# A decoder block with its first query's rope moved into the pair slots, and three other changes of order

## The chip, the cores and the metric

The kernel runs on one core of one Trainium2 chip. The metric is the device time of one execution in microseconds. The kernel before was timed in three runs: median 942.23 us, lowest 941.05, highest 942.41. A profiler's trace of one further execution comes with it. TensorE multiplies matrices, VectorE and ScalarE work on elements, GpSimd (POOL in the profile) does a little of both, and SyncE (SP) only issues transfers. Each engine works through its own list of instructions in order and waits at semaphores for the others.

## The reference, cut to what matters

One layer on x of 1024 positions by 1024 channels, all in float32. A modulated RMSNorm gives h; one input projection of h is split into parts; two branches are gated, projected, merged, projected again and added to x; a last RMSNorm ends it.

```python
h = rmsnorm(x, norm_g) * (1.0 + scale) + shift          # scale, shift, gate = c @ w_ada + b_ada
q, k, v, g_attn, xr, g_rnn, m_attn, m_rnn = split(h @ w_in)
q, k = partial_rope(q, positions), partial_rope(k, positions)   # 16 of 64 channels turned
y_attn = sliding_window_attention_with_sinks(q, k, v, sinks) * silu(g_attn)   # 16 heads, 4 kv heads, window 128
xr = causal_depthwise_conv(xr, conv_w, conv_b)                    # width 4
y_rnn = rg_lru(xr, positions, wa, ba, wx, bx, lam) * silu(g_rnn)  # a linear scan over positions
merged = sigmoid(m_attn) * (y_attn @ w_attn_proj) + sigmoid(m_rnn) * (y_rnn @ w_rnn_proj)
out = rmsnorm(x + gate * (merged @ w_out), final_g)
```

## The kernel before, in words

**Precision.** TensorE's fast float32 format keeps fewer bits than float32. So each operand is split into a high part (a cast, on ScalarE: `cast`, line 101 or, with a scale, 103) and a low part (the operand minus the high part, on VectorE: `rest`, line 107 or 109). A product is three matmuls: high by high, low by high, high by low. In the profile `wh` and `wl` are the two parts of a weight; `hh`, `hl` and `nh`, `nl` those of h and of differences of its blocks.

**Start.** Norm and modulation give h transposed, in eight chunks of 128 channels (`kc`). Three column blocks of the input projection (`starts`: two blocks of k, one of the first query q 0) are accumulated meanwhile. From there to the end of the attention the order is written by hand: the instructions of each engine run in the order of the Python code. Behind the start come: rope of the k blocks (`rope_a` for the block with the turned channels, `rope_b` for the other), the product for v (`v_product`, its results stored by `v_store`), the rope of the third start block, the split of the weights `rq[1]` of the second half of q 0, the operands `nh`, `nl` (`make_operands`), and the product of the second half of q 0 (`ps_q`), which needs both halves of those weights (`wq`).

**Pairs and slots.** The remaining columns of the input projection are 23 pairs of column blocks, in the order of the list `pairs`: Q[1], MA[0], Q[2], MA[1], Q[3], XR[0], and so on (Q: queries, MA and MR: merge gates, XR: the recurrent branch, GA and GR: SiLU gates). A pair is computed by Strassen's scheme: seven block products instead of eight, one in each of seven slots, every product 12 matmuls of 128x128 by 128x512 (line 506). Pair i starts at slot 7 i. `Pair.place` writes down in which slots the pair's other steps are issued: four transfers of weights from six slots before its start; sums of weight blocks (`tsum`) and the splits (`hi` on ScalarE, `lo` on VectorE) from two slots before; evacuations of the four PSUM banks; and the results' own steps (`sinks`: for a query, rope and stores to the DRAM tensors `q_d`; for gates, tanh and stores). A split is written one slot ahead of the product that uses it or earlier. `at_slot` appends steps to the list of a slot (`fixed`), so that in one slot the steps of the earlier pair stand ahead of those of the later one. Rope is two ScalarE copies of 32 rows and a VectorE product (f1), a product and a sum of 64 rows (f2), a cast (`rhi`) and a subtraction (`rlo`), the last two also for blocks that are not turned; then two stores on SP's queue.

**Background.** Work that no slot needs is kept in two waiting lists and issued by `background` when a planner's account of ScalarE and VectorE time (each step carries its estimated costs, `Load`) has room in the slot. `slots(n)` in such a list holds it for n slots. The first list has the gate row (`gate_row`: eight pieces of `w_gate`, multiplied and added on VectorE, summed by TensorE) and then the steps behind the recurrent gates (`after_gates`: sigmoids a1, a2, d1, d2, tanh a3, a4, a5, d3, root a6, d4, scan d5, d6, a7, d7; a is ScalarE, d VectorE). The second has the preparation of v (`v_prep`, four groups) and then the convolutions. There are four recurrent blocks (`hb` 0 to 3) with two halves each; in `start_gates` a `slots(1)` stands behind each step for hb 0 to 2, and behind step 0 alone for hb 3. The gate products of the recurrent blocks are inserted between slots on TensorE (`extra`).

**Attention and output.** The 32 blocks of attention start in slot 155, with the last pair and the first output projections as filling work. After them the written order ends, and the compiler's scheduler orders the rest by its own estimate of times, with program order as priority: the projection of the attention output with the merge, the preparation of the output weights (`load_wo`: load, multiply by the gate, split; `wo[k]` for k 0 to 7, with two buffers for the loaded piece), and the output product. For the first three of the eight output tiles the product (`out_k`, line 1511, six matmuls for a tile and a k) runs in chunks of k.

Of the kernel before, what the change touches and what calls it, by code (L numbers as in the profile page):

```python
# [23 lines left out]
S = 1024  # L24
D = 1024
# [26 lines left out]
def tile_hybrid_block(ctx, tc, x, pk, rows, posr, posi, invf, c_row, w_ss, w_gate, w_main, w_v,  # L52
# [42 lines left out]
    def slot():  # L95
        return (wp.tile([P, HALF], F32R, tag="wh", name="wh", bufs=5),
                wp.tile([P, HALF], F32R, tag="wl", name="wl", bufs=5))
# [14 lines left out]
    def split(dst, src, scale=1.0):  # L112
        cast(dst, src, scale)
        rest(dst, src, scale)
        return dst
# [271 lines left out]
    def make_operands(i):  # L387
        for t in (i, i + 4):
            nl[t] = hx.tile([P, S], F32R, tag="X", name="nl")
            A.copy(nh[t][:], xT[t][:])  # L390
            V.tensor_tensor(out=nl[t][:], in0=xT[t][:], in1=f32(nh[t][:]), op=ALU.subtract)
        NT1.append((nh[i][:, SL[0]], nl[i][:, SL[0]]))
        NT3.append((nh[i][:, SL[1]], nl[i][:, SL[1]]))
        NT4.append((nh[i + 4][:, SL[0]], nl[i + 4][:, SL[0]]))
        T2.append((nh[i + 4][:, SL[1]], nl[i + 4][:, SL[1]]))
# [56 lines left out]
    def now(*lists):  # L452
        for steps in zip(*lists):
            for st_ in steps:
                st_[3]()
# [27 lines left out]
    def slots(d):  # L483

        t = []

        def f():
            t.append(W["slot"])
            return W["slot"] >= t[0] + d
        return f  # L490

    def at_slot(t, *steps):

        for i, st_ in enumerate(steps):
            for one in st_ if isinstance(st_, list) else [st_]:
                fixed.setdefault(t + i, []).append(one)


    SLOT, GATE = 2.75, 5.5

# [9 lines left out]
    class Pair:  # L510
        def __init__(self, c, sinks, scale=1.0):
            self.c, self.sinks, self.scale = c, sinks, scale

        def place(self, s, par, last):

            b1, b2, b3 = bk[0], bk[1 + par], bk[3]
            R, O, sc = {}, {}, self.scale
            self.ops, self.banks = O, (b1, b2, b3, bk[2 - par])

            def load(n):  # L520
                i, j = int(n[1]) - 1, int(n[2]) - 1
                return "S", 0, 0, lambda: R.__setitem__(
                    n, load_half(w_main[self.c + i][:, SL[j]]))

            def tsum(dst, a, b, op):
                def f():
                    R[dst] = wp.tile([P, HALF], F32, tag="ws", name="ws", bufs=3)[:]
                    V.tensor_tensor(out=R[dst], in0=R[a], in1=R[b], op=op)  # L528
                return "D", 0, 0.69, f

            def hi(n):
                def f1():
                    O[n] = slot()
                    cast(O[n], R[n], sc)
                return "A", 0.62, 0, f1

            def lo(n):
                return "D", 0, 0.69, lambda: rest(O[n], R[n], sc)

            SUB, ADD = ALU.subtract, ALU.add  # L540
            at_slot(s - 6, [load("A11"), load("A21")], load("A22"), load("A12"))
            at_slot(s - 2, [hi("A11"), tsum("S1", "A21", "A22", ADD)],
                    [hi("S1"), lo("A11"), tsum("S2", "S1", "A11", SUB)],
                    [lo("S1"), tsum("S3", "A21", "A11", SUB)],
                    hi("S2"),
                    [hi("A12"), lo("S2"), tsum("S4", "S2", "A12", SUB)],
                    [hi("S4"), lo("A12")], [hi("S3"), lo("S4")], lo("S3"))
            at_slot(s + (5 if last else 7), hi("A22"), lo("A22"))

            T_ = {}  # L550

            def keep(n, src):
                def f():
                    T_[n] = stp.tile([P, HALF], F32, tag=n, name=n)
                    A.copy(T_[n][:], src)
                return "A", 0.58, 0, f

            at_slot(s + 1, ("A", 0.58, 0, lambda: A.copy(b1, b2)))
            at_slot(s + 2, keep("p5", b3))
            at_slot(s + 4, keep("u2", b2))  # L560
            at_slot(s + 5, *self.sinks["C11"](lambda: b1))

            def join(out_, n, a, b):
                def f():
                    T_[n] = out_()
                    V.tensor_tensor(out=T_[n], in0=a(), in1=b(), op=SUB)
                return "D", 0, 0.69, f

            d12, k12 = self.sinks["C12"]
            d22, k22 = self.sinks["C22"]  # L570
            at_slot(s + 6, join(d12, "C12", lambda: T_["u2"][:], lambda: b3),
                    *k12(lambda: T_["C12"]))
            at_slot(s + 7, join(d22, "C22", lambda: b2, lambda: T_["p5"][:]),
                    *k22(lambda: T_["C22"]))
            if last:
                def add():
                    V.tensor_tensor(out=T_["u2"][:], in0=T_["u2"][:], in1=self.banks[3], op=ADD)
                at_slot(s + 7, keep("u2", b2), ("D", 0, 0.69, add),
                        *self.sinks["C21"](lambda: T_["u2"][:]))
            else:  # L580
                at_slot(s + self.sinks.get("late", 10), *self.sinks["C21"](lambda: b2))
# [40 lines left out]

    def place(pairs):
        for i, p in enumerate(pairs):
            p.place(7 * i, i % 2, i == len(pairs) - 1)

    def run(pairs, extra):

# [126 lines left out]
    def start_gates(hb):  # L755

        load1, split1 = gate_weights(hb, 1)
        c0, c1 = after_gates(hb, 0), after_gates(hb, 1)
        waiting[0].append(lambda: ask(hb, 0))
        one, two = [], [lambda: ask(hb, 1)]  # L760
        for todo, steps_ in ((one, c0), (two, c1)):
            for i, step in enumerate(steps_):
                todo.extend(step + ([slots(1)] if hb < 3 or i == 0 else []))
                if todo is one and i == 1:
                    todo.append(lambda: second(hb))
        if hb == 3:
            one.insert(0, lambda: W.setdefault("rush", True))
        waiting[0].extend(one + two)
        waiting[1].extend([load1, slots(2)] + split1)
        return True  # L770
# [89 lines left out]
    def gate_row():  # L860
# [7 lines left out]
        def start():  # L868
            t["acc"] = gm.tile([P, D], F32, name="acc")
            load(0)  # L870
            load(1)
# [55 lines left out]
                                   op1=ALU.add)  # L927
            V.memset(pcol(PK_NG, 0), 1.0)

        start()  # L930
        waiting[0].append(slots(5))
        todo = [[("A", 1.5, 0, lam_a)], [("D", 0, 1.0, lam_0)]]
        todo += [[("D", 0, 1.05, lambda j=j: [lam_j(j - i) for i in range(3)])]
                 for j in (8, 5, 2)]
# [9 lines left out]
    def v_prep(g):  # L944
        t = {}
        vpp = W["vpp"]

        def f0():
            t["v"] = vpp.tile([P, 8, 64], F32, tag="v32", name="v32")
            dma(t["v"][:], v_d[:, :, g, :])  # L950

        def f1():
            t["d"] = vpp.tile([P, 8, 64], F32, tag="d32", name="d32")
            V.tensor_tensor(out=t["d"][:, 1:8, :], in0=t["v"][:, 1:8, :],
                            in1=t["v"][:, 0:7, :], op=ALU.subtract)
            V.tensor_copy(t["d"][:, 0, :], t["v"][:, 0, :])

        def f2():
            for n_ in ("vs", "dv"):
                t[n_] = vpp.tile([P, 8, P], F32R, tag=n_, name=n_)  # L960
            A.copy(t["vs"][:, :, 0:64], t["v"][:])
            A.copy(t["dv"][:, :, 0:64], t["d"][:])

        def f3():
            for n_, d_, dst in (("v", "vs", vs_d), ("d", "dv", dv_d)):
                V.tensor_tensor(out=t[d_][:, :, 64:128], in0=t[n_][:],
                                in1=f32(t[d_][:, :, 0:64]), op=ALU.subtract)
                dma(dst[g], t[d_][:])

        waiting[1].extend([[("S", 0, 0, f0)], slots(4 if g else 7), [("D", 0, 0.85, f1)],  # L970
                           [("A", 1.24, 0, f2)], [("D", 0, 1.38, f3)]])


# [320 lines left out]
    def part(i, rope, dst):  # L1294
        return [rope(lambda hf=hf: starts[i][1][hf], hf, dst) for hf in range(2)]
# [1 line left out]
    now(*part(0, rope_a, k_d))  # L1297
    v_product(bk[:2], 0)
    now(*part(1, rope_b, k_d))
    now(*part(2, rope_a, q_d[0]))  # L1300
    ps_v = new_ps()
    v_product(ps_v, 1)
    wq.append(split(slot(), rq[1], 0.125))
    v_store(bk[:2], 0)
    make_operands(0)
    make_operands(1)
    begin(-4, -3, -2)
    make_operands(2)
    v_store(ps_v, 1)
# [2 lines left out]
    ps_q = new_ps()  # L1312
    for kc in range(KC):
        mm_k(ps_q, wq, kc)
    now(*[rope_b(lambda hf=hf: ps_q[hf], hf, q_d[0]) for hf in range(2)])
    T.matmul(bk[0], hh[0][0][:, 0:P], hh[0][0], start=True, stop=True)
    b12_ctx.close()
    Load.act = Load.dve = 0.0
# [229 lines left out]
    for t in range(3):  # L1548
        load_x(t)
    first = [new_ps() for _ in range(3)]  # L1550
    for lo, hi in ((0, 4), (4, 8)):
        for t in range(3):
            for k in range(lo, hi):
                out_k(first[t], t, k)
# [91 lines left out]
```

## Time and profile before

| | |
|---|---|
| Median of three runs | 942.23 us |
| Lowest, highest | 941.05, 942.41 us |
| The profiled execution | 944.67 us |
| Its span, from first to last instruction | 942.9 us |
| Mean granted TensorE clock | 0.995 |
| TensorE busy | 910.3 us (97%) |
| VectorE busy | 688.4 us (73%) |
| ScalarE busy | 532.3 us (56%) |
| GpSimd busy | 109.1 us (12%) |
| DMA, mean over the span | 174 GB/s |

Times in the rows of a profile are microseconds from the start of the span. In a row of instructions stand the start, the duration, the engine, the source line, the operation, what it writes and reads with their shapes, and in brackets the time that the engine sat idle before it and what it waited for. Matmuls are pipelined: the time between two starts is what one costs, not its duration. PEld is the loading of weights, SPq SyncE's issuing of transfers. PEclk is the share of full clock that TensorE was granted.

### The profile page before, as it was taken

Reading aid. Unit: us, or ns where it says so; the run is one execution under the profiler, and the core shown is the slowest. Engines: PE = TensorE matmul, PEld = TensorE weight load, DVE = VectorE, ACT = ScalarE, POOL = GpSimd, SP = SyncE. Lnnn points to the kernel's source line nnn. Section 1 sums busy time; section 2 is a strip of 40 time slices with the busy share of each in tenths; the row PEclk is TensorE's granted clock in tenths of the full one; section 3 lists DMA queues with packets and bytes.
Section 4 is the critical chain, followed back from the end, with each engine's and each line's share of the span. In section 5 each row is a group of like instructions: output and inputs, shape, how many; then the busy total and the mean of one; then the engine's idle time right before and its main releaser. Section 6 shows DMA issues by size and latency. Waiting matters only on the chain. (4 is left out here: it accounts for less than half of the span.)

```text
span 942.9 us, 12429 instructions
## 1 busy us (share of the span) xinstructions
PE 910.3 (97%) x4261; PEld 753.2 (80%) x4261; DVE 688.4 (73%) x1068; ACT 532.3 (56%) x1038; POOL 109.1 (12%) x161
## 2 busy tenths in 40 slices
PE   5899989999999999999999999999999999998997
PEld 3689777788888888888887877888888888887886
DVE  8977798876668974986687675899999736656522
ACT  7434655454557755775687685888878622212311
POOL 1056000000000000000000001354454300000000
PEclk9999999999999999999999999999999999999999
DMA  8924565753323451354235348996655186436321
GB/s 318 364 68 155 181 223 201 268 181 130 115 79 122 144 181 34 124 176 155 71 134 190 100 152 266 325 350 210 215 186 175 57 323 225 164 126 211 124 78 67
DMA packets 81140, 164.20 MB, mean 174 GB/s; under 512 B 12771, under 2 KB 29155, under 8 KB 81078
## 3 DMA queue, kind: packets, MB, share of 16 engines
q1 hardware_dynamic: 77590, 155.06, 47.9%
q0 software_dynamic: 2192, 6.00, 2.0%
q10 hardware_dynamic: 1296, 2.36, 0.7%
q8 instruction: 33, 0.54, 0.2%
q14 instruction: 29, 0.24, 0.1%
HBM read 114.00 MB, written 49.78 MB: 174 GB/s over the span
## 5 line engine op out<-in xcount | busy, mean ns | idle before, releaser
L506 PE MATMUL bk<-nh,wl 128*128 128x512 f32 x368 | 144.6, 393 | 2.8 <-DVE wl L107 2.7
L506 PE MATMUL bk<-nh,wh 128*128 128x512 f32 x368 | 144.2, 392 | 0.0
L506 PE MATMUL bk<-nl,wh 128*128 128x512 f32 x368 | 143.8, 391 | 0.0
L107 DVE TENSOR_TENSOR wl<-r,wh 128x512 fp32r<-128x512 f32 x108 | 79.4, 739 | 17.8 <-ACT wh L101 17.8
L101 ACT CAST wh<-r 128x512 fp32r<-128x512 f32 x108 | 66.4, 619 | 33.5 <-DMA r<-w_ap 12.5
L506 PEld LDWEIGHTS bk<-nh,wl 128*128 128x128 f32 x368 | 69.5, 189 | 19.4 <-DVE wl L107 4.5
L506 PEld LDWEIGHTS bk<-nh,wh 128*128 128x128 f32 x368 | 69.4, 188 | 15.4 <-ACT wh L103 0.9
L506 PEld LDWEIGHTS bk<-nl,wh 128*128 128x128 f32 x368 | 69.5, 189 | 14.2
L506 PE MATMUL bk<-hh,wl 128*128 128x512 f32 x184 | 71.8, 390 | 1.1 <-DVE wl L107 1.1
L506 PE MATMUL bk<-hh,wh 128*128 128x512 f32 x184 | 71.6, 389 | 0.0
L506 PE MATMUL bk<-hl,wh 128*128 128x512 f32 x184 | 71.6, 389 | 0.0
L59 POOL DMA_DIRECT2D yh_d<-yh x1 | 0.6, 583 | 480.4 <-ACT yh L845 480.4
L107 DVE TENSOR_TENSOR wl<-ws,wh 128x512 fp32r<-128x512 f32 x80 | 54.4, 686 | 1.9 <-ACT wh L101 1.9
L101 ACT CAST wh<-ws 128x512 fp32r<-128x512 f32 x80 | 48.4, 614 | 5.9 <-DVE ws L528 4.6
L1050 ACT ACTIVATE p<-p,small 128x129 f32<-128x129 f32 x128 | 50.1, 401 | 0.0
L506 PEld LDWEIGHTS bk<-hh,wl 128*128 128x128 f32 x184 | 34.5, 188 | 8.9 <-DVE wl L107 1.9
L506 PE MATMUL bk<-hha,wl 128*128 128x512 f32 x92 | 36.1, 393 | 5.2 <-DVE wl L107 3.7
L506 PEld LDWEIGHTS bk<-hh,wh 128*128 128x128 f32 x184 | 34.5, 188 | 7.2
L506 PEld LDWEIGHTS bk<-hl,wh 128*128 128x128 f32 x184 | 34.5, 188 | 7.1
L1026 PE MATMUL s_ps<-ks,qs 128*128 128x256 f32 (+1 forms) x256 | 37.6, 289 | 0.2 <-DVE p L1040 0.2
L1528 ACT ACTIVATE o<-xo 128x1024 f32<-128x1024 f32 (+2 forms) x10 | 8.9, 889 | 48.7 <-DVE xo L1527 48.7
L506 PE MATMUL bk<-hla,wh 128*128 128x512 f32 x92 | 35.8, 389 | 0.0
(356 smaller groups left out, 2260.3 us busy)
## 6 DMA issues: line engine op xcount, KB each, us to landing
r<-w_main SPq DMA_DIRECT2D x100, 256.0 KB, 4.2
wada<-w_ss SPq DMA_DIRECT2D x16, 512.0 KB, 8.1
qs<-q_d SPq DMA_DIRECT2D x16, 512.0 KB, 5.5
ks<-k_d SPq DMA_DIRECT2D x24, 192.0 KB, 3.8
xt<-x SPq DMA_DIRECT2D x8, 512.0 KB, 7.0
q_d<-rhi SPq DMA_DIRECT2D x16, 256.0 KB, 3.7
q_d<-rlo SPq DMA_DIRECT2D x16, 256.0 KB, 3.0
wg<-w_gate SPq DMA_DIRECT2D x8, 512.0 KB, 5.6
```

What stands on the lines that cost most here:

```text
L59: return eng.dma_start(dst, src)
L101: A.copy(dst[0][:], src)
L107: V.tensor_tensor(out=dst[1][:], in0=src, in1=f32(dst[0][:]), op=ALU.subtract)
L506: W["pe"] = T.matmul(ps, ww[:, c], b[kc][xx_], start=(first and kc == 0 and i == 0), stop=(kc == 3 and i == 2), skip_group_check=not first)
L1026: W["pe"] = T.matmul(o, qs[:, j, qc], ks[:, b, k0 + (0 if n else P):k0 + 256], start=(b == 0), stop=(b == 1))
L1050: A.activation(px[:, j, :], px[:, j, :], AF.Exp, bias=sm[:, 0, j:j + 1], accum_out=sm[:, 1, j:j + 1])
L1528: A.activation(o[:, sl], xo[:, sl], AF.Square, accum_out=fs[:, i:i + 1])
```

## The change

Five edits, all of them of order. The third start block's rope is not run at once; its two halves are copied out of PSUM (two ScalarE copies) and their rope steps are put in slots 1 to 5; the rope of the second half of q 0 goes to slots 5 to 7. The split of `rq[1]` moves behind the first stores of v and two calls of `make_operands`. The weight steps of a pair that follows a query (pairs 1, 3 and 5) are put in front of what their slots hold (`ahead`). The gate row's first transfers are issued four slots later, and its first step waits three slots more instead of five in all; v's first transfer is four slots later and its wait four instead of seven. In the last recurrent block a `slots(1)` stands behind steps 0, 3 and 5 of the first half and 0, 3, 5 and 7 of the second. The first three output tiles go in chunks of k 0-1, 2-3 and 4-7 instead of 0-3 and 4-7.

```diff
+    def ahead(t, *steps):
+        for i, st_ in enumerate(steps):
+            fixed.setdefault(t + i, [])[:0] = st_ if isinstance(st_, list) else [st_]
...
-        def place(self, s, par, last):
+        def place(self, s, par, last, put_):
...
-            at_slot(s - 2, [hi("A11"), tsum("S1", "A21", "A22", ADD)],
+            put_(s - 2, [hi("A11"), tsum("S1", "A21", "A22", ADD)],
...
-            p.place(7 * i, i % 2, i == len(pairs) - 1)
+            p.place(7 * i, i % 2, i == len(pairs) - 1,
+                    ahead if i and pairs[i - 1] in Q else at_slot)
...
-                todo.extend(step + ([slots(1)] if hb < 3 or i == 0 else []))
+                gap = hb < 3 or i in ((0, 3, 5) if todo is one else (0, 3, 5, 7))
+                todo.extend(step + ([slots(1)] if gap else []))
...
-        start()
-        waiting[0].append(slots(5))
+        waiting[0].extend([slots(4), [("S", 0, 0, start)], slots(3)])
...
-        waiting[1].extend([[("S", 0, 0, f0)], slots(4 if g else 7), [("D", 0, 0.85, f1)],
+        waiting[1].extend(([] if g else [slots(4)]) + [
+                           [("S", 0, 0, f0)], slots(4), [("D", 0, 0.85, f1)],
...
-    now(*part(2, rope_a, q_d[0]))
+    kept = [blk(), blk()]
+    for hf in range(2):
+        A.copy(kept[hf], starts[2][1][hf])
+        at_slot(hf + 1, *rope_a(lambda hf=hf: kept[hf], hf, q_d[0]))
     ps_v = new_ps()
     v_product(ps_v, 1)
-    wq.append(split(slot(), rq[1], 0.125))
     v_store(bk[:2], 0)
     make_operands(0)
     make_operands(1)
+    wq.append(split(slot(), rq[1], 0.125))
...
-    now(*[rope_b(lambda hf=hf: ps_q[hf], hf, q_d[0]) for hf in range(2)])
+    for hf in range(2):
+        at_slot(hf + 5, *rope_b(lambda hf=hf: ps_q[hf], hf, q_d[0]))
...
-    for lo, hi in ((0, 4), (4, 8)):
+    for lo, hi in ((0, 2), (2, 4), (4, 8)):
```

More of the change, by code (lines that the diff above doesn't have):

```diff
@@ L541, in place @@
             at_slot(s - 6, [load("A11"), load("A21")], load("A22"), load("A12"))
-            at_slot(s - 2, [hi("A11"), tsum("S1", "A21", "A22", ADD)],
[L543 to L547, printed above, removed]
+            put_(s - 2, [hi("A11"), tsum("S1", "A21", "A22", ADD)],
+                 [hi("S1"), lo("A11"), tsum("S2", "S1", "A11", SUB)],
+                 [lo("S1"), tsum("S3", "A21", "A11", SUB)],
+                 hi("S2"),
+                 [hi("A12"), lo("S2"), tsum("S4", "S2", "A12", SUB)],
+                 [hi("S4"), lo("A12")], [hi("S3"), lo("S4")], lo("S3"))
             at_slot(s + (5 if last else 7), hi("A22"), lo("A22"))
```

## The prediction

> **What bounds the kernel now.** I read the page's busy table first, then the list of who made TensorE wait, then TensorE's instructions in order of time, then the granted clock in short stretches.
>
> ```profile
> span 942.9 us, 12429 instructions
> PE 910.3 (97%) x4261; PEld 753.2 (80%) x4261; DVE 688.4 (73%) x1068; ACT 532.3 (56%) x1038; POOL 109.1 (12%) x161
> ...
> PE bk L506 <- DVE wl L107: 7.5, 5, 2.4
> ...
> PE rp L1511 <- ACT wo L1446: 2.4, 1, 2.4
> PE bk L506 <- DVE wl L109: 1.5, 1, 1.5
> ```
>
> TensorE is the bound. Its matmuls are the same before and after, so the change can only win or lose time that TensorE waits. After the first 50 us nearly all of that is a matmul waiting for the low part of a split weight (wl, from VectorE) and one wait for an output weight (wo). In order of time, the number in brackets being the idle time:
>
> ```profile
> 99.16 0.39 PE L506 MATMUL bk<-hha,wh 128*128 128x512 f32 x1
> 101.06 0.50 PE L506 MATMUL bk<-hha,wl 128*128 128x512 f32 x1 [1.51 <-DVE wl L109]
> ...
> 117.72 0.39 PE L506 MATMUL bk<-hha,wh 128*128 128x512 f32 x1
> 120.48 0.50 PE L506 MATMUL bk<-hha,wl 128*128 128x512 f32 x1 [2.37 <-DVE wl L107]
> 120.82 0.40 PE L506 MATMUL bk<-hla,wh 128*128 128x512 f32 x1
> 121.05 0.39 PE L506 MATMUL bk<-hha,wh 128*128 128x512 f32 x1
> ...
> 160.17 0.49 PE L506 MATMUL bk<-hha,wl 128*128 128x512 f32 x1 [1.32 <-DVE wl L107]
> ...
> 557.73 0.50 PE L506 MATMUL bk<-nh,wl 128*128 128x512 f32 x1 [2.30 <-DVE wl L107]
> ...
> 569.12 0.50 PE L506 MATMUL bk<-hh,wl 128*128 128x512 f32 x1 [1.11 <-DVE wl L107]
> ...
> 851.27 0.73 PE L1511 MATMUL rp<-wo,hh 128*128 128x512 f32 x2 [2.41 <-ACT wo L1446]
> ```
>
> Undisturbed matmuls start 0.23 us apart (120.82, 121.05), so a pair slot of twelve is 2.72. The wait at 120.48 costs (120.48 - 117.72 - 0.23) + (0.34 - 0.23) = 2.64, its idle time plus 0.27; I price every wait so. Two of them leave a second bill, in the column PEclk of these windows:
>
> ```profile
> 120.00:125.00 5.00, 4.52 (x20) 3.75 (x21) 5.00 (x8) 3.48 (x7) 0.00 (x0) 1.00 0.24 95
> ...
> 559.00:562.50 3.50, 3.50 (x10) 2.68 (x9) 2.78 (x4) 3.47 (x6) 0.00 (x0) 0.51 0.41 118
> ...
> 852.50:856.00 3.50, 3.50 (x10) 2.70 (x9) 2.78 (x3) 1.10 (x2) 0.00 (x0) 0.51 0.70 246
> ```
>
> Behind 557.73 and 851.27 about 3.4 us run at half clock, some 1.6 us lost each; behind 120.48, as long a wait, the clock stayed at 1.00. By the Trainium skill, "TensorE: Matmul & The Clock Gate", Part 1, half rate comes after at least one idle window of about 3.4 us, in windows that run free of the kernel. By that rule none of these waits is long enough and the two bills of 1.6 would stay whatever becomes of the waits; the trace disagrees, with half clock after idle times of 2.30 and 2.41, and I go by the trace. That the windows run free would fit the spared wait at 120.48.
>
> Bills: 101.06 1.78; 120.48 2.64; 160.17 1.59; 557.73 2.57 + 1.6; 569.12 1.38; 851.27 2.68 + 1.6. Together 15.8.
>
> **Part 1, the first query's rope, the gate weights and the order of the weight steps** (waits at 101, 120 and 160). The rope of query 0 now stands ahead of the low part that slot 0 waits for:
>
> ```profile
> 84.71 0.68 DVE L427 TENSOR_TENSOR c<-bk,ctab 128x512 f32<-128x512 f32 x1
> ...
> 89.65 1.50 DVE L446 TENSOR_TENSOR rlo<-c,rhi 128x512 fp32r<-128x512 f32 x2
> ...
> 92.90 4.63 DVE L391 TENSOR_TENSOR nl<-xT,nh 128x1024 fp32r<-128x1024 f32 x4 [1.15 <-ACT nh L390]
> ...
> 100.32 0.68 DVE L109 SCALAR_TENSOR_TENSOR wl<-r,wh 128x512 fp32r<-128x512 f32 x1
> ```
>
> The eight VectorE instructions from 84.71 to 91.15 leave: 6.4 us. Two ScalarE copies of about 0.58 (half a bank each, as its other evacuations) come in. The chain then is bound by ScalarE's casts, and the low part is ready some 4 to 5 us sooner, at about 96, before slot 0 asks at 99.4. The wait of 1.78 goes. Moved behind eight operand casts is the split of rq[1]: by the same rows it ends near 92.5, and the query's matmuls, 48 at 0.227 ending at 99, want it at their half, 93.7. That is the thinnest margin here, 1 us. In slots 1 to 7 VectorE gets the 6.4 us and the two rope_b halves (1.3) back, about 20 us of work for slots 1 to 9, which last 21.8; in slots 5 and 6 MA[0]'s weights now stand first, so what is late next is the rope, and nobody on TensorE waits for that.
>
> The wait at 120.48 is a transfer, held on SP's queue:
>
> ```profile
> 105.71 0.32 SPq L59 DMA_DIRECT2D q_d<-rlo  x1
> ...
> 108.80 2.40 SPq L59 DMA_DIRECT2D r<-w_main x4
> ...
> 115.24 0.62 ACT L101 CAST wh<-r 128x512 fp32r<-128x512 f32 x1 [1.59 <-DMA r<-w_main]
> ...
> 116.56 0.69 DVE L528 TENSOR_TENSOR ws<-r 128x512 f32<-128x512 f32 x1 [2.18 <-DMA r<-w_main]
> ...
> 159.44 0.68 DVE L107 TENSOR_TENSOR wl<-r,wh 128x512 fp32r<-128x512 f32 x1
> ```
>
> The four weight loads of pair 1 stand behind the stores of query 0 (waiting for rlo), two gate-weight loads of 512 KB and v. After the change the stores are issued in slots 4 to 7, the gate weights and v in slot 4, behind those loads; SP issues them near 95 to 100, ten us earlier. The wait of 2.64 goes. SP now blocks in slots 4 to 7 on rlo, but the next loads behind it are pair 2's in slot 8, wanted in slot 12, 11 us later. At 160 the low part of 159.44 stood behind rope f2 (two instructions) and a join, 2 us; with the weights first it ends near 157, slot 21 asks at 158.7. 1.59 goes. Price of part 1: 6.0 of gain, with 0 to -1 for the rq[1] margin; I take -6.0. Working the planner's own costs slot by slot, the gate row's sum reaches TensorE in slot 34 instead of 28 and ends in slot 38, the last v step in 39, one slot before XR[0] takes the rope's memory. Its four matmuls only move: nothing.
>
> **Part 2, gaps in the last block** (waits at 558 and 569):
>
> ```profile
> 541.10 1.23 DVE L842 TENSOR_TENSOR rz<-rz,gg 128x1024 f32<-128x1024 f32 x1 [1.17 <-DMA gg<-sgr_d]
> ...
> 555.84 1.23 DVE L826 SCALAR_TENSOR_TENSOR th<-rz,th 128x1024 f32<-128x1024 f32 x1 [2.88 <-ACT rz L823]
> 556.99 0.69 DVE L107 TENSOR_TENSOR wl<-r,wh 128x512 fp32r<-128x512 f32 x1
> ...
> 562.07 2.29 DVE L838 TENSOR_TENSOR_SCAN rz<-av,it 128x1024 f32<-128x1024 f32 x1
> ...
> 568.39 1.29 DVE L107 TENSOR_TENSOR wl<-ws,wh 128x512 fp32r<-128x512 f32 x2
> ```
>
> VectorE sat 2.88 us before d3 with the wanted low part queued behind it. By the planner's costs d3 goes from slot 147 to 148, behind that low part; d4 and the scan from 148/149 to 150, d6 and d7 from 150 to 151/152. The gate products stay in slots 138 and 143, and attention still opens in slot 155 (the lists now empty in 152, before in 150). So 557.73 and its half clock go: 4.2. But TensorE then arrives 4.6 earlier at the low part of 568.39, which stands behind the scan: a6 ends near 560.6 (its casts and a table load after 555.8), d4 1.15, scan 2.2, low part 0.7: 564.7, and TensorE asks near 563.3. A wait of 1.4 stays there, and smaller ones in slots 148, 153 and 154 (S1, S3 and the next A11 behind d2, d6 and d7) come to about 0.9. Left 2.3 of the 5.55: I take -3.2. Bounds: 0 (the waits only move) and -5.5 (all go).
>
> **Part 3, output chunks in twos** (wait at 851):
>
> ```profile
> 844.62 1.07 PE L1511 MATMUL rp<-wo,hha 128*128 128x512 f32 x4
> ...
> 863.23 0.61 PE L1511 MATMUL rp<-wo,hh 128*128 128x512 f32 x2
> ...
> 876.60 0.62 PE L1511 MATMUL rp<-wo,mh 128*128 128x512 f32 x2
> ...
> 851.25 1.22 DVE L1447 TENSOR_TENSOR wo<-wo,wo 128x1024 fp32r<-128x1024 f32 x1 [1.17 <-ACT wo L1446]
> ...
> 859.13 1.05 ACT L1446 CAST wo<-wo 128x1024 fp32r<-128x1024 f32 x1 [3.09 <-DVE wo L1443]
> ...
> 874.00 2.48 DVE L1447 TENSOR_TENSOR wo<-wo,wo 128x1024 fp32r<-128x1024 f32 x2
> ```
>
> With k 0 and 1 of three tiles first, 36 matmuls (8.2 us) run before wo[2] is wanted: at 852.8, and both its parts are there at 852.5. The 4.3 go at first. But the chain that makes wo[3] to wo[7] does not depend on TensorE, and the order behind the 54th matmul stays, I expect. wo[3] is cast at 860.2; its first matmul, the 64th, would now come at 858.9 instead of 863.23: a wait of 1.3. The low part of wo[6] is ready at about 875.2, and its first use was at 876.60: TensorE cannot be more than 1.4 earlier there. I take -1.4, between 0 (the order behind changes for the worse) and -4.3.
>
> Sum: -6.0 - 3.2 - 1.4 = -10.6. The profiled execution took 944.67 (span 942.9 and 1.8 around it); that becomes 934.1. The median of the runs is 942.23, 2.4 below the profiled one, and becomes 931.6.
>
> **The rivals.** (a) All the waits go, those at the ends of parts 2 and 3 too: -15.8, 926.4. For it: the remaining waits are differences of 1 to 2 us between long chains; against it the rows at 562.07 and 874.00. (b) Parts 2 and 3 give nothing, the gaps and the chunks only moving the waits: 936.2. (c) A remaining wait meets the half clock again; one or two stretches of 1.6: 933.2 to 934.8. The row at 120.48 shows that a wait need not meet it. By the same section of the Trainium skill, windows running free of the kernel, no run need repeat another in this; no run here shows that yet. (d) Slower: the rope's ring. The rhi and rlo tiles have two buffers, and a cast into one waits until its store of two halves ago has landed, 3.7 us from issue:
>
> ```profile
> q_d<-rhi SPq DMA_DIRECT2D x16, 256.0 KB, 3.7
> ```
>
> Eight halves now pass in slots 3 to 12, four of them new. If each held ScalarE for the whole landing, 30 us, less some 6 of slack there, MA[0]'s and Q[2]'s casts would come late and TensorE lose about 24: 942.2 - 10.6 + 24 = 956. It decides from 10.6 us of loss, 2.1 held per half with the slack. Against it: by the rows above a half is issued every 2.7 us, so a store has about 5 us to land, and I find waits of 1 us or less. (e) Nothing: the low parts are late for another reason behind the removed one, in all three places; within 1.9 of 942.2.
>
> **Chances.** The sum as worked 0.45; (b) 0.17; (c) 0.12; (a) 0.12; (d) 0.07; (e) 0.07. Range 925.5 to 937.5: it takes in (a) to (c), leaves out (d) and (e); around the likeliest alone 928 to 934. About 0.2% (1.9 us) is what a measurement of this kernel can tell from no change: faster 0.86, same 0.06, slower 0.08.
>
> **What would show it.** Right: no idle TensorE above 0.4 us between 62 and 500 but for the place of 505; the weight loads of pair 1 issued before 101; no half clock near 559 and 853; a wait of about 1.4 in slot 152 behind the scan; in the output waits at wo[3] and wo[6] of 1 to 1.5 each. Wrong: a wait near 93 inside the query's matmuls (rq[1]), rhi casts idle for q_d stores, or an output order that differs after its first 54 matmuls.

## The result, and the profile after

The changed kernel took 937.05 us (median of 5 runs, 936.33 to 938.61) beside 942.23: the ratio is 0.9951, 95% interval 0.9937 to 0.9966. It is faster by 5.2 us in medians and by 7.6 between the two profiled executions (944.67 and 937.05). The forecast was 931.6, a gain of 10.6; the time lies at the upper end of its range, nearest to rival (b).

First who made TensorE wait, in the changed kernel. Columns: the matmul that waited, whom it waited for, us in total, times, the longest.

```profile
span 935.3 us, 12434 instructions
PE 908.0 (97%) x4261; PEld 752.4 (80%) x4261; DVE 688.0 (74%) x1068; ACT 533.7 (57%) x1040; POOL 109.0 (12%) x161
...
PE bk L511 <- DVE wl L107: 5.4, 5, 2.6
...
PE rp L1522 <- DVE wo L1458: 0.7, 1, 0.7
```

Before, waits for low parts were 9.0 us in six; now 5.4 in five, and the wait of 2.4 for an output weight has become 0.7. In order of time these are the matmuls that wait (the number in brackets), with the granted clock of two stretches (column PEclk, the third number from the end) below:

```profile
499.24 0.50 PE L511 MATMUL bk<-nh,wl 128*128 128x512 f32 x1 [0.37 <-DVE wl L107]
538.67 0.50 PE L511 MATMUL bk<-hh,wl 128*128 128x512 f32 x1 [0.85 <-DVE wl L107]
547.81 0.50 PE L511 MATMUL bk<-nh,wl 128*128 128x512 f32 x1 [0.68 <-DVE wl L107]
559.89 0.50 PE L511 MATMUL bk<-hh,wl 128*128 128x512 f32 x1 [0.90 <-DVE wl L107]
565.53 0.68 PE L511 MATMUL bk<-nh,wl 128*128 128x512 f32 x1 [2.63 <-DVE wl L107]
868.87 0.74 PE L1522 MATMUL rp<-wo,mh 128*128 128x512 f32 x2 [0.70 <-DVE wo L1458]
```

```profile
566.00:569.50 3.50, 3.50 (x10) 2.73 (x9) 3.08 (x5) 1.79 (x4) 2.51 (x5) 0.56 0.93 315
852.50:856.00 3.50, 3.50 (x17) 2.92 (x16) 1.50 (x2) 1.05 (x1) 0.00 (x0) 1.00 0.53 167
```

Nothing waits any more near 101, 120 and 160. In the last recurrent block there were two waits; now there are four, in slots 145, 148, 152 and 153, the last with a half-clock stretch behind it.

To place the gain I took, in every trace of this study, the times between the starts of certain matmuls (us, my subtraction): slot 0 to slot 136 (where part 1 acts), slot 136 to 155 (the gaps), slot 155 to 161 (attention's first block), slot 161 to the output product, and the output's first 128 matmuls (the chunks). The rest of the span is the same in all to within 0.9.

| kernel | 0-136 | 136-155 | 155-161 | 161-out | out 128 |
|---|---|---|---|---|---|
| before | 409.23 | 68.81 h | 24.81 | 242.61 | 33.34 h |
| before, second trace | 410.65 h | 69.20 | 24.81 | 242.67 | 30.73 |
| changed | 402.72 | 70.61 h | 24.81 | 242.67 | 30.41 |
| changed, second trace | 402.77 | 71.27 h | 24.81 | 242.65 | 30.24 |
| part 1 only | 402.75 | 68.73 h | 24.81 | 246.65 h | 30.31 |
| gaps only | 410.73 h | 71.10 h | 24.80 | 243.21 | 30.71 |
| chunks only | 410.39 h | 69.29 | 24.80 | 242.59 | 29.91 |
| no gaps | 402.75 | 69.03 h | 24.81 | 243.45 | 29.93 |
| gap before d3 only | 402.72 | 69.28 h | 24.81 | 242.85 | 30.52 |
| gg late, no gaps | 402.76 | 70.89 h | 24.81 | 242.63 | 30.28 |
| gg early, gaps | 402.75 | 64.41 | 26.58 | 243.62 | 29.53 |
| the same, second trace | 402.74 | 64.41 | 28.58 h | 242.21 | 31.39 |
| gg early, no gaps | 402.75 | 67.71 | 24.81 | 243.28 | 29.87 |
| the same, second trace | 402.72 | 67.26 | 24.81 | 242.80 | 29.86 |

An h marks a stage with a stretch of about 3.4 us at half clock, some 1.6 us lost. So, by the first traces, part 1 gained 6.5, the gaps lost 1.8, the output gained 2.9 against this one trace of before and 0.3 against its second.

### The profile page after: what moved, and what is told of

Read it like the earlier page. It is cut to its first block, busy times and chain, and to the rows that moved or that the text cites. A ratio compares the mean times of both kernels' runs of the same rounds, so it can differ in the third digit from the quotient of the medians.

```text
span 935.3 us, 12434 instructions
## 1 busy us (share of the span) xinstructions
PE 908.0 (97%) x4261; PEld 752.4 (80%) x4261; DVE 688.0 (74%) x1068; ACT 533.7 (57%) x1040; POOL 109.0 (12%) x161
## 4 chain that ended last, share of the span: by engine, by line
PE 75%; DVE 10%; DMA 6%; ACT 5%; issue 4%; SPq 0%; POOL 0%; ACTq 0%; DVEq 0%
PE bk L511 41%; PE rp L169 9%; PE pmain L169 4%; PE pgate L794 4%; PE rp L1522 3%; PE pmain L1522 3%; PE s_ps L1033 3%; PE pv L1105 2%; DMA wo<-w_out 2%; DMA tt<-tr_d 1%; PE pt L1071 1%; DVE wl L107 1%; PE bk L169 1%; DMA smr<-smr_d 1%; DVE wo L1458 1%
## 5 line engine op out<-in xcount | busy, mean ns | idle before, releaser
L511 PE MATMUL bk<-hha,wh 128*128 128x512 f32 x92 | 35.9, 391 | 0.0
```

The lines of the kernel that those rows point to most:

```text
L511: W["pe"] = T.matmul(ps, ww[:, c], b[kc][xx_], start=(first and kc == 0 and i == 0), stop=(kc == 3 and i == 2), skip_group_check=not first)
```

## The experiments

Every ratio is to the kernel before, timed on the same chip in the same series; the intervals are 95%.

**1. Each part alone, and all but the gaps.** The first kernel has only the edits of rope, weight order and gate weights, the second only the gaps, the third only the chunks.

> The rope, weight-order and gate-weight edits alone (gaps and chunks as before). Theory: the three waits near 101, 120 and 160 us go and nothing else changes, 6.5 us by the two traces; in runs 6 to 7 us faster than before (ratio 0.993). Rival: the traces differ by 7.6 us over the span but the medians by 5.2, so part of the early lead is eaten elsewhere even without the gaps; then 4 us or less.

> The gaps in the last recurrent block alone. Theory: the load of gg moves behind a tanh store and a weight load on SP's queue, d6 comes late with a wanted low part behind it, and the kernel gets slower by 1 to 2 us (the lead of the changed kernel fell from 6.5 to 4.7 us there). Rival: the gaps win by themselves (about 3 us, as predicted) and only lose beside part 1.

> The output chunks of two alone. Theory: the wait for wo[2] and the half clock behind it go and under 1 us comes back at wo[6] and wo[7]: 2.9 us faster by the traces. Rival: the half clock behind the wait is not there in most runs, and the gain is 1.5 us.

The fourth is the changed kernel with the old line for the gaps:

```diff
-                gap = hb < 3 or i in ((0, 3, 5) if todo is one else (0, 3, 5, 7))
-                todo.extend(step + ([slots(1)] if gap else []))
+                todo.extend(step + ([slots(1)] if hb < 3 or i == 0 else []))
```

> The changed kernel with the gaps of the last block taken back. Theory: 9.4 us faster than before (6.5 + 2.9), 1 to 2 us faster than the changed kernel. Rival (the gaps help as predicted): slower than the changed kernel by 3 us.

Beside 942.53 for before: part 1 only 936.35, ratio 0.9938 (0.992 to 0.9956); gaps only 943.94, 1.0024 (1.0009 to 1.0039); chunks only 942.26, 0.9993 (0.9982 to 1.0004); no gaps 935.22, 0.9922 (0.9906 to 0.9939). So part 1 gives 6.2, as forecast. The gaps cost 1.4 alone, clear of noise, and 1.8 beside the rest, where the intervals just touch (0.9937 to 0.9966 for the changed kernel): the sign of that term was wrong. The chunks give 0.3 alone and 1.1 beside part 1 (part 1 only against no gaps); both lie within the intervals, so no gain of theirs is shown. Two expectations missed for that reason: chunks only did not gain 2.9 or 1.5, and no gaps gained 7.3 in place of 9.4.

**2. Why the gaps lose: gg.** Step d4 ends by issuing the load of gg, which d6 needs. VectorE and SP in the changed kernel's trace, second half of the last block:

```profile
555.70 1.23 DVE L840 SCALAR_TENSOR_TENSOR it<-th,it 128x1024 f32<-128x1024 f32 x1 [1.89 <-ACT th L837]
556.96 2.29 DVE L845 TENSOR_TENSOR_SCAN rz<-av,it 128x1024 f32<-128x1024 f32 x1
559.17 0.66 DVE L107 TENSOR_TENSOR wl<-ws,wh 128x512 fp32r<-128x512 f32 x1
563.65 1.22 DVE L849 TENSOR_TENSOR rz<-rz,gg 128x1024 f32<-128x1024 f32 x1 [3.82 <-DMA gg<-sgr_d]
564.80 0.68 DVE L107 TENSOR_TENSOR wl<-ws,wh 128x512 fp32r<-128x512 f32 x1
...
557.61 0.33 SPq L59 DMA_DIRECT2D smr_d<-c  x1
558.03 0.39 SPq L59 DMA_DIRECT2D r<-w_main  x1
558.50 0.41 SPq L59 DMA_DIRECT2D gg<-sgr_d  x1
```

The same place before:

```profile
559.72 1.23 DVE L833 SCALAR_TENSOR_TENSOR it<-th,it 128x1024 f32<-128x1024 f32 x1 [2.05 <-ACT th L830]
560.87 0.68 DVE L107 TENSOR_TENSOR wl<-ws,wh 128x512 fp32r<-128x512 f32 x1
561.47 0.69 DVE L528 TENSOR_TENSOR ws<-ws,r 128x512 f32<-128x512 f32 x1
562.07 2.29 DVE L838 TENSOR_TENSOR_SCAN rz<-av,it 128x1024 f32<-128x1024 f32 x1
564.27 0.67 DVE L107 TENSOR_TENSOR wl<-r,wh 128x512 fp32r<-128x512 f32 x1
564.85 1.22 DVE L842 TENSOR_TENSOR rz<-rz,gg 128x1024 f32<-128x1024 f32 x1
...
560.98 0.33 SPq L59 DMA_DIRECT2D gg<-sgr_d  x1
```

Before, gg was issued 0.03 us after d4's end (560.95), and d6 found it there. With the gaps, d4 falls in a slot where a tanh store and a weight load stand ahead of gg on SP's queue: it is issued 1.57 after d4's end (556.93) and the data comes 5.15 later. The two VectorE instructions between d4 and the scan now run ahead of d4, so d6 is also at the head of VectorE's list sooner. It waits 3.82, with the low part of 564.80 queued behind it; TensorE waits for that at 565.53. Theory 1 is this late load; its rival, theory 2, is that the gaps set d4 to d7 against wanted low parts wherever gg is loaded.

Early load, one step ahead, in a tile of its own (the second kernel also without the gaps):

```diff
         def d3():
...
+            if hb == 3:
+                t["gg"] = W["rn"].tile([P, S], F32, tag="xc", name="gg", bufs=2)
+                dma(t["gg"][:], sgr_d[c])
...
         def d4():
...
-            dma(tl("gg", "th"), sgr_d[c])
+            if hb < 3:
+                dma(tl("gg", "th"), sgr_d[c])
```

> The changed kernel, but in the last block gg has a tile of its own and is loaded one step earlier, right behind d3, ahead of the tanh store and the weight load that it stands behind on SP's queue in the changed kernel. Theory 1: the late load of gg holds d6 on VectorE (idle 3.87 and 3.82 us there), with a wanted low part queued behind it. Then the waits in slots 145 and 153 (0.85 and 2.63 us, and the half clock behind the second) go: 1.1 + 2.9 + 1.6 = 5.6 us less than the changed kernel, 931.5; the wait of 0.9 in slot 152 behind the scan stays. Rival, theory 2: the gaps themselves put d4 to d7 against wanted low parts, wherever gg is loaded; then 936 to 937 as the changed kernel.

> The changed kernel without its gaps in the last block, and with gg loaded one step earlier into a tile of its own. Theory 1: without the gaps gg was not late for any wanted low part, so this equals the kernel without gaps, 935.2, within 1 us; the early load pays only beside the gaps. If the early load frees VectorE earlier there too (d6 sat 1.2 us for gg in the first half): 934. Theory 2: 935.2, and the kernel with gaps and the early load is slower than this by 1.5 to 2.

Old place, on GpSimd's queue:

```diff
-            dma(tl("gg", "th"), sgr_d[c])
+            dma(tl("gg", "th"), sgr_d[c], G if hb == 3 else nc.sync)
```

> The changed kernel, but in the last block gg is loaded in its old place (step d4) on GpSimd's queue, past the store and the weight load on SP's. Theory 1 with the hold on SP alone to blame (1.6 us from d4's end to gg's issue): d6 starts 1.6 us earlier and the wait in slot 153 shrinks from 2.6 to about 1.1, perhaps without half clock: 934 to 935.5. If the landing itself (about 5 us) is to blame: little less than the changed kernel, 936 to 937. Theory 2 (the gaps themselves): 937.

One slot more between the load and d6 (a hold behind step 6, added in the first half and in place of the one behind step 7 in the second):

```diff
-                gap = hb < 3 or i in ((0, 3, 5) if todo is one else (0, 3, 5, 7))
+                gap = hb < 3 or i in ((0, 3, 5, 6) if todo is one else (0, 3, 5, 6))
```

> The changed kernel with the last block's gap behind its seventh step instead of the last, so that one slot more lies between gg's load (d4) and its use (d6), in both halves. Theory 1: the wanted low part of slot 153 comes ahead of d6, gg has landed by then, and the waits of slots 145 and 153 go as with the early load: 931.5 to 934, with d6 and d7 now a slot later and what follows them perhaps late by up to 1.5. Theory 2: the waits move by a slot, 936 to 938.

Beside 942.62 for before: early load 934.1, ratio 0.9912 (0.9895 to 0.9928); early load without gaps 934.07, 0.9911 (0.9895 to 0.9927); GpSimd's queue 937.59, 0.9945 (0.9928 to 0.9963); gap before d6 933.77, 0.9903 (0.9885 to 0.992). With the early load the waits in slots 145 and 153 are gone, as theory 1 has it, and the one in slot 148 too; only the one behind the scan stays, 1.14 at 558.16. The time falls between the two theories: 934.1, clearly below the changed kernel and not the 931.5 of theory 1. The table shows one loss against that, 1.8 in slots 155 to 161. VectorE at the wait that stays:

```profile
555.23 2.29 DVE L849 TENSOR_TENSOR_SCAN rz<-av,it 128x1024 f32<-128x1024 f32 x1
557.43 0.67 DVE L107 TENSOR_TENSOR wl<-ws,wh 128x512 fp32r<-128x512 f32 x1
558.02 1.22 DVE L853 TENSOR_TENSOR rz<-rz,gg 128x1024 f32<-128x1024 f32 x1
```

Here d6 (558.02) starts without idle time; in the changed kernel VectorE idled 3.82 us before it.

On GpSimd's queue gg was issued 0.3 us after d4's end and came 4.8 later; the wait in slot 153 fell from 2.63 to 1.03, as expected of the hold alone. The times do not follow: its profiled execution took 934.65, the others 937.0 to 938.96. Half clock is not enough to explain it: three of the others have the mean granted clock of the profiled one, 0.998, and took 937.0, 937.12 and 938.96. What they lose and that one did not is open.

**3. The parts of part 1, and second traces.**

> The changed kernel unaltered, as the base for the two below and for a second trace of it. All theories: 936 to 938, waits in slots 145, 148, 152 and 153 as in the first trace (0.85, 0.7, 0.9, 2.6 us). If half-clock stretches belong to the execution and not to the kernel, the one behind the wait in slot 153 may be gone or stand elsewhere; if they belong to the wait, it stands there again.

> The kernel before unaltered, for a second trace of it and for what two sets of times of one kernel differ by. All theories: 942.2 to 942.9. The prediction took the two half-clock stretches (behind 557.73 and 851.27, 1.6 us each) and the wait of 2.41 us for wo as lasting bills. If they come and go, this trace lacks one or more of them and its span lies nearer to the median (940.5); if they are fixed, they stand again at the same places.

```diff
-                    ahead if i and pairs[i - 1] in Q else at_slot)
+                    at_slot)
```

> The changed kernel, but with every pair's weight steps placed at their slots as before, not in front of the rope's. By the prediction's part 1 the wait of 1.32 us near 160 comes back (1.6 us), and in slots 5 and 6 MA[0]'s weights stand behind the moved rope, with up to 2 us there: 938.6 to 940.6 beside 937.0 for the changed kernel. Rival: the order counts for nothing once the rope is moved, 937.

```diff
-        waiting[0].extend([slots(4), [("S", 0, 0, start)], slots(3)])
+        start()
+        waiting[0].append(slots(5))
...
-        waiting[1].extend(([] if g else [slots(4)]) + [
-                           [("S", 0, 0, f0)], slots(4), [("D", 0, 0.85, f1)],
+        waiting[1].extend([[("S", 0, 0, f0)], slots(4 if g else 7), [("D", 0, 0.85, f1)],
```

> The changed kernel, but the gate weights and v are loaded at once as before, not four slots on. By the prediction the wait near 120 came from the stores of query 0 at the head of SP's queue; with these gone to slots 4 to 7 the two gate loads and v alone delay pair 1's weight loads by at most their issue and transfer, some 4 us of the 10 gained, and no wait comes back: 936.5 to 938. Rival: the gate loads are what held pair 1's weights, and the wait of 2.4 comes back, 939.7, with half clock 941.

Beside 941.63 for before: changed again 937.44, 0.9953 (0.994 to 0.9967); before again 942.55, 1.0005 (0.9995 to 1.0016), which shows what one kernel differs by from itself; old weight order 939.61, 0.9979 (0.9968 to 0.9991); gate weights at once 936.99, 0.9952 (0.9936 to 0.9968). The weight order is worth 2.2, inside what was expected, and the trace has waits near 160 again:

```profile
155.39 0.50 PE L511 MATMUL bk<-hha,wl 128*128 128x512 f32 x1 [0.68 <-DVE wl L107]
...
158.88 0.50 PE L511 MATMUL bk<-nh,wl 128*128 128x512 f32 x1 [0.43 <-DVE wl L107]
```

The later gate weights are worth nothing by themselves. SP's queue with them at once, and in the changed kernel:

```profile
99.64 1.54 SPq L59 DMA_DIRECT2D wg<-w_gate  x2
...
102.09 2.15 SPq L59 DMA_DIRECT2D r<-w_main  x4
```

```profile
93.57 4.74 SPq L59 DMA_DIRECT2D r<-w_main  x4
```

Pair 1's weights are issued at 102.09 instead of 93.57, still 6.7 ahead of the 108.80 of before, and nobody waits near 120. It was the stores of query 0 that held them.

**4. What the gaps are worth without the late load.** The early load left the kernels with and without gaps at the same time (934.1 and 934.07). Four kernels: only the gap ahead of d3, which is what the forecast counted on; a late load without any gap; and the two early ones once more on one chip.

```diff
-                gap = hb < 3 or i in ((0, 3, 5) if todo is one else (0, 3, 5, 7))
+                gap = hb < 3 or i in (0, 3)
```

> The changed kernel, but of its gaps in the last block only the one ahead of d3 is kept (none ahead of d4, none ahead of the copy of yh). This is what the prediction counted on: d3 behind the wanted low part. Theory 1 (gg's late load took the gain): d4 and gg's load move one slot less than with all gaps; if gg's issue is no longer behind the tanh store, the loss goes and the gain of the first gap stays: 932.5 to 934.5. Theory 2 (any gap moves a wait on to the next low part): 935 to 937.

```diff
         def d4():
...
-            dma(tl("gg", "th"), sgr_d[c])
+            if hb < 3:
+                dma(tl("gg", "th"), sgr_d[c])
...
         def d5():
...
+            if hb == 3:
+                dma(tl("gg", "th"), sgr_d[c])
```

> The changed kernel without its gaps in the last block, and with gg's load there issued one step later, behind the scan's step instead of d4's. No gap moves any step of VectorE; gg alone comes later by 0.5 to 2.5 us. Theory 1: d6 waits for gg again (it did not in the second half without gaps) and the low part behind it is late: 936 to 938 beside 935.2 without gaps. Theory 2: the load's place counts for nothing, 935.

> The kernel with the early load of gg and all the gaps, once more, beside the next one on the same chip. Its first profile was 1.5 us under the median of its other runs. If the gaps gain once gg is early, as the prediction's mechanism has it: 932 to 934 and 1 to 2 us under the next kernel. If they only move the waits: equal to it, 934.

> The kernel with the early load of gg and no gaps, once more, for the same comparison: 934 in both cases; waits of 1.4, 0.9, 0.4 and 1.1 us near 551 to 562 as in its first trace, with or without a half-clock stretch behind one of them.

Beside 941.67 for before: the one gap 934.69, 0.9923 (0.9909 to 0.9936); late load without gaps 937.22, 0.995 (0.9938 to 0.9963); early load with gaps 934.42, 0.9918 (0.9905 to 0.9932); early load without gaps 933.17, 0.9909 (0.9895 to 0.9922).

The late load costs without any gap: 937.22 beside 935.22 (no gaps; the ratios' intervals, 0.9938 to 0.9963 and 0.9906 to 0.9939, overlap by 0.0001). The two waits that it adds, 0.69 and 0.75 in slots 145 and 147, come to 2.0 with the 0.27 that the prediction adds to each idle time. Moved behind the scan's step, it too falls behind the tanh store and the weight load:

```profile
531.30 0.33 SPq L59 DMA_DIRECT2D smr_d<-c  x1
531.67 0.42 SPq L59 DMA_DIRECT2D r<-w_main  x1
532.19 0.41 SPq L59 DMA_DIRECT2D gg<-sgr_d  x1
...
536.65 1.23 DVE L851 TENSOR_TENSOR rz<-rz,gg 128x1024 f32<-128x1024 f32 x1 [3.22 <-DMA gg<-sgr_d]
...
538.53 0.50 PE L511 MATMUL bk<-hh,wl 128*128 128x512 f32 x1 [0.69 <-DVE wl L107]
```

In the changed kernel that row of SP stands at 532.17 and the matmul's wait is 0.85. So theory 1's mechanism is enough for the loss. But theory 2 has a share in the missing gain: the one gap's 934.69 is not clearly below no gaps' 935.22 and lies between what the two theories expected, and with gg early the gaps still give nothing in the time, 934.42 beside 933.17. The trace of the one gap shows one reason:

```profile
554.62 1.23 DVE L840 SCALAR_TENSOR_TENSOR it<-th,it 128x1024 f32<-128x1024 f32 x1 [2.49 <-ACT th L837]
555.88 2.29 DVE L845 TENSOR_TENSOR_SCAN rz<-av,it 128x1024 f32<-128x1024 f32 x1
558.09 0.67 DVE L107 TENSOR_TENSOR wl<-r,wh 128x512 fp32r<-128x512 f32 x1
...
558.81 0.79 PE L511 MATMUL bk<-hh,wl 128*128 128x512 f32 x1 [4.11 <-DVE wl L107]
```

The wait behind d3 is gone, and one of 4.11 stands behind d4 (idle 2.49 for the root) and the scan; without gaps there were two, 2.34 and 1.07. The waits only merged. With all gaps and gg early, slots 136 to 155 do take 2.8 to 3.3 us less than with gg early alone (table), but slots 155 to 161 then take 1.8 and 3.8 more in the two traces, the second with a half-clock stretch. That TensorE reaches attention too early would fit; in the second trace, TensorE and ScalarE there:

```profile
590.35 0.47 PE L1109 MATMUL pv<-phc,vs 128*128 128x512 f32 x1 [1.46 <-ACT phc L1080]
...
588.19 0.33 ACTq L59 DMA_DIRECT2D smr_d<-c  x1
588.61 0.37 ACT L1118 COPY ob<-pv 64x256 f32<-64x256 f32 x1 [3.42 <-DMA r<-w_rp]
...
589.38 0.59 ACT L1080 CAST phc<-pt 128x512 fp32r<-128x512 f32 x1
```

ScalarE stands 3.42 us, by the trace for a transfer, with the cast that TensorE wants behind it. The gap before d6 gives back more there (29.95 in place of 24.81, waits of 2.08 at 582.61 and 1.50 at 592.87) after the shortest stage 136 to 155 of all, 63.53. Why ScalarE is held was not tried.

## Why the prediction was right or wrong

**Part 1, forecast -6.0: right.** -6.2 in the times, -6.5 in the traces (409.23 to 402.72), where all three waits are gone. Pair 1's loads are issued at 93.57, before 101. The margin of rq[1] held, no wait near 93. One sign that I had named for rival (d) did appear, a cast of rhi waiting for a store, and for 4.88 us where I had found 1 or less:

```profile
117.46 0.59 ACT L442 CAST rhi<-pmain 128x512 fp32r<-128x512 f32 x1 [4.88 <-DMA q_d<-rhi]
```

ScalarE had so much to spare there: no matmul between 62 and 499 waits over 0.3 us, and (d), which needed 10.6 us of TensorE, did not come. The old weight order costs 2.2 in the times and 2.4 in the traces, beside 1.59 in the forecast, with up to 2 more in slots 5 and 6. The gate weights' delay was not part of that price and is worth nothing.

**Part 2, forecast -3.2: the failed step, +1.8 in its place.** d3 did go behind its low part and the wait at 558 went; the wait of 1.4 expected behind the scan came as 0.90 in slot 152. What failed is "smaller ones in slots 148, 153 and 154 ... come to about 0.9": slot 145 waits 0.85, slot 148 0.68, slot 153 2.63, the last with a half-clock stretch of 1.6. I moved d4 to another slot and did not follow the load that it issues past SP's queue there, though the row of d6 waiting for gg stood in the prediction. That load, issued 1.57 us behind d4 in place of 0.03, held d6 for 3.82 us with the wanted low part behind it. The bound "0 (the waits only move)" was wrong for the same cause: nothing excluded a loss. One figure of the step does not add up either: TensorE arrives "4.6 earlier" where 4.2 was taken away; with 4.2 the wait behind the scan comes to 1.0, nearer to the 0.90. And even with gg early the term would have been about 0: the waits merge (gap before d3 only), or the time is given back at attention's start, where the cause is not shown.

**Part 3, forecast -1.4: not shown in the times.** -0.3 alone, -1.1 beside part 1, both within the intervals; the wait for wo[2] did go. Waits at wo[3] and wo[6] were expected at 1 to 1.5 each; there is one of 0.70 and one of 0.07. The bill of 4.3 for wo[2] was not a lasting one. In the second trace of the kernel before the matmul that waited 2.41 waits 0.06, since TensorE reaches the output 1.9 us later while wo[2] is multiplied and cast only 0.4 sooner; a transfer sets that:

```profile
848.44 1.23 DVE L1443 TENSOR_TENSOR wo<-wo,gate_bc 128x1024 f32<-128x1024 f32 x1 [3.38 <-DMA wo<-w_out]
...
849.76 1.05 ACT L1446 CAST wo<-wo 128x1024 fp32r<-128x1024 f32 x1 [5.50 <-DVE wo L1443]
```

In the first trace these rows stand at 848.86 and 850.17. So a delay of TensorE elsewhere is partly paid back here, and the old order had less to give than one trace showed (33.34 for 128 matmuls, 30.3 to 30.7 in three other traces with the old order).

**The profiled execution and the median.** The forecast carried the difference of 2.4 to the median and held the half-clock stretches of that execution for bills that the edits would take away. They come and go. The second trace of the kernel before has the stretch behind the wait near 120, where the first had none, and none behind the wait near 559, where the first had one:

```profile
120.33 0.50 PE L506 MATMUL bk<-hha,wl 128*128 128x512 f32 x1 [2.10 <-DVE wl L107]
...
559.61 0.50 PE L506 MATMUL bk<-nh,wl 128*128 128x512 f32 x1 [2.35 <-DVE wl L107]
```

Most of what decides can be read from the traces' record of the granted clock. In every trace it changes only at times that lie whole multiples of 3.413 us apart, and a stretch lasts one such step: in the first trace of before from 558.99 to 562.40 and from 852.54 to 855.95, the two starts 293.55 apart, which is 86 steps. TensorE's busy time and granted clock (the third number from the end) in such steps, first trace, then second:

```profile
118.67:122.08 3.41, 1.60 (x7) 1.00 0.64 225
...
555.58:558.99 3.41, 1.26 (x5) 1.00 0.45 133
558.99:562.40 3.41, 3.41 (x10) 0.50 0.41 117
```

```profile
118.34:121.75 3.41, 1.42 (x6) 1.00 0.58 205
121.76:125.17 3.41, 3.41 (x9) 0.50 0.07 26
...
555.25:558.66 3.41, 2.01 (x9) 1.00 0.16 60
558.66:562.07 3.41, 2.46 (x11) 1.00 0.68 216
```

A half-clock stretch follows a step that is idle for long enough, not a wait that is long enough. Between 62 and 915 us of the eighteen traces every one of the 13 steps with 1.82 us or more of idle time was followed by a stretch, and none with 1.64 or less; of the three between, 1.66 and 1.67 were and 1.81 was not. The wait of 2.30 near 558 had 2.15 in one step; the one of 2.35 in the second trace fell into two, 1.41 and 0.94, and met no half clock; of the 2.37 at 120.48 that was spared, 1.81 fell into one. Where the steps lie against the kernel differs from one execution to the next, so whether a given wait of some 2 us meets half clock is luck. This is read off the traces; no run set it.

The prediction weighed the Trainium skill, "TensorE: Matmul & The Clock Gate", Part 1. That windows run free of the kernel agrees with these rows: the same wait met half clock in one execution and not in another. That an idle window of about 3.4 us is needed does not: 1.82 us (chunks only, near 120) were enough.

**Rivals.** (b) gave 936.2 and came nearest, but by a loss in part 2, not by a nothing there; what part 3 gave is not shown. (c) did come, behind the wait in slot 153, in both traces of the changed kernel.

**The sum.** -6.2 - 1.1 + 1.8 = -5.5 goes from before over part 1 only and no gaps to the changed kernel, so it closes by construction, but for 0.3 between two series of runs. The three parts each alone make a sum of their own: -6.2 + 1.4 - 0.3 = -5.1, beside -5.2 measured. The kernel without the gaps is faster than the changed one, and the fastest that were tried have the early load, with or without gaps (933.17 to 934.42), or the gap before d6 (933.77): 2.6 to 4.3 below the changed kernel's 937.05 and 937.44. Between them the runs do not decide.

## What to carry to other kernels

When a step is moved, list every transfer that it issues and look at what stands on that queue at its new place; a load that was issued 0.03 us after its step can be issued 1.6 us after it, and its user then holds everything queued behind it. A wait that is removed is worth only the distance to the next one on the same chain, so price the next low part (here d4's idle time and the scan) before the gain is booked. Take the bills of a single trace as one sample: a wait against a transfer's arrival, and half clock behind a wait, differed here from one execution to the next by more than the output's edit was worth.

## What the runs showed of the hardware

Half clock (a granted clock of 0.50) lasted 3.41 us and began only on a grid of 3.413 us steps, and, between 62 and 915 us, behind a step in which TensorE had been idle for at least 1.66 us; 1.82 or more was always enough in these traces, 1.64 or less never. I had taken it as fixed to the wait. Waits of 2.35 and 2.56 met none, since they were split between two steps (1.41 and 0.94; 1.60 and 0.96); a wait of 1.59 met one, with 1.66 idle in its step. In the same place of the changed kernel it came in both traces (2.63), but in two of five executions of its first series the mean granted clock was 0.999, as in the trace with the early load that has no such stretch, beside 0.996 in the traced ones. Why 1.81 was spared and 1.66 was not is open.

A load of 512 KB issued behind two other transfers on SP was used 5.15 us after its issue (changed kernel, 558.50); on the same queue, issued without them ahead, it was there within 3.87 us (before, 560.98).
